# A hybrid attention encoder layer: eight landing buffers for stored block sums and u, low parts in halves, a merge ordered by token halves, and the second batch's mask loaded into memory that the first batch's u leaves

## The chip, the cores and the metric

The kernel runs on one core of one Trainium2 chip. The metric is the time of one execution on the device in microseconds (us), the median of several runs. Three runs of the kernel before gave 1134.05, 1135.88 and 1137.46 us; the median is 1135.88 us.

## The reference, cut to what matters

One encoder layer is applied to two request batches, the prompt (512 tokens) and the sample (1024 tokens), with the same weights, in float32. `D_MODEL` is 1024, and there are eight heads of 64 in each of two attention branches.

```python
def encoder_layer(x, ...):
    h = rmsnorm(x, norm_g)
    proj = h @ w_in                       # qa ka va za qb kb vb zb ga gb
    ...
    oa = neighbourhood_attention(qa, ka, va, rpb_a) * jax.nn.silu(za)   # window of 8 x 16 grid neighbours, bias per offset
    oa = oa @ w_o_a
    ob = window_gqa_attention(qb, kb, vb, t5_table, sink_b) * jax.nn.silu(zb)   # |i-j| <= 128, T5 bias, sink logit
    ob = ob @ w_o_b
    merged = jax.nn.sigmoid(ga) * oa + jax.nn.sigmoid(gb) * ob
    return x + merged @ w_out
```

`qa`, `ka`, `qb`, `kb` are normalised per head before the attention. In the kernel, u is the attention output times silu(z); g is the sigmoid of a gate.

## The kernel before

**Precision.** TensorE multiplies float32 operands that are split in two: a high part (the value as ScalarE writes it in the matmul's format) and a low part (the value minus the high part). Each product is three matmuls, high by high, high by low, low by high. ScalarE makes the high part (`whi`, `hh`, `T` first of a pair), VectorE or GpSimd the low part (`wlo`, `hl`, `T` second). Both parts of a pair of `T` tiles have the name `T` in the profile. So every operand passes DMA, then ScalarE, then VectorE or GpSimd, and then TensorE.

**Stages.** For each batch: norm, attention in six head groups (lines 607 to 1104: `att_weights`, `tables`, `project`, `make_qk`, `attend`, `weigh`), then `dense_phase`: z, the gates g, the merge with w_o_a and w_o_b, and the output product. The prompt's stages come first, and some of the sample's norm is done beside the prompt's dense phase. In the traced execution the prompt's attention runs to about 217 us, its dense phase to about 395 us, the sample's attention to about 785 us, and the sample's dense phase to the end.

**Attention.** `att_weights` loads four tiles of 768 columns for each group into `w` (the tag `w32`, two buffers), and makes `whi` and `wlo` of them; one instruction makes the whole low part. `project` multiplies h by them into a bank `p`; from it come the sums of squares, `rs_v` and `rs_r` on GpSimd, then `qk` on VectorE (line 816), which TensorE transposes (line 861). `tables` makes a table `bias` out of `mask` (one load, line 671) and `raw` (a load for each head, line 682) on VectorE or GpSimd (line 695). The scores need the table.

**Dense phase.** For the sample, z, g and the output use Strassen's seven products in place of eight (`pair_strassen`). Its operands from h are differences of four blocks of h. These block sums were stored to memory (`t_d`) beside the prompt's work and come back through `stored_sums`: each of 16 pieces is loaded to a landing buffer `U` (four buffers) and split into `T`. The u of each head pair, 16 pieces of 512 tokens, is stored to `u_d` and comes back through `split_u`, over two `fr` and two `ot` buffers. The merge takes the eight output blocks m and, inside each, the two token halves n, and needs u of that half. `fill_gates` are products of some gates that need only h; they are strewn into the sample's attention (`fh`, `fl`, bank `d`) to give TensorE something to do.

**What sets the order.** Every operation is put on record with a priority, its engine or choice of two engines, and the tiles that it makes and uses. `Flow.run` is a planner: with fixed cost formulas it plays the program through, and issues for each engine the ready operation with the smallest priority whose buffers are free. Where an operation may go to VectorE or GpSimd, it takes the one that it expects to end it sooner; operations with `port` don't overlap between those two engines in its plan. The order it finds is the program's: each engine takes its instructions strictly in that order, and waits where an operand or a buffer isn't there. The SyncE queue (SP) issues all DMAs in one order too, so a DMA that waits for its buffer or for the value it stores holds up all behind it.

**Memory.** `Stage` is a pool that is opened when others have been closed. The sample's `early` pool holds its q, k and small tiles and opens where the prompt's `u_p` was; its `late` pool holds `mask`, `raw`, `bias` and the rest of its attention, and opens when `norm_s`, `d1_p`, `rb`, `d0_p` and the prompt's h are closed.

Of the kernel before, what the change touches and what calls it, by code (L numbers as in the profile page):

```python
# [34 lines left out]
RAW = {512: 2, 1024: 1}  # L35
# [5 lines left out]
P = 128  # L41
# [313 lines left out]
def encoder_kernel(  # L355
# [238 lines left out]
    def att_weights(src, n, prio, engs=("pool", "dve"), place=None, after=()):  # L594

        st, at, new = place or (f.value(wpool, [P, 768], F32, "w32", W32), 0, True)
        hi = f.value(wpool, [P, 768], F32R, "whi", 6)
        lo = f.value(wpool, [P, 768], F32R, "wlo", 6)
        sv = lambda: st.t[:, at : at + n]
        ld = f.dma(lambda: nc.sync.dma_start(sv(), src), 512 * n, prio, after=after, **({"new": [st]} if new else {"hold": [st]}))  # L600
        a = f.op(
            (("act", ACT_(n) + 40),), lambda e: act.activation(hi.t[:, :n], sv(), AF.Copy),
            prio, new=[hi], hold=[st], after=[ld],
        )

        def emit(e):
            engines[e].tensor_tensor(lo.t[:, :n], sv(), hi.t[:, :n].bitcast(F32), op=ALU.subtract)
# [40 lines left out]
    def attention_phase(geo, hh, hl, h_ops, mask_d, early, late):  # L648
# [6 lines left out]
        def tile_(shape, dt, tag, bufs):  # L655
            return f.value(early if tag in ("sq", "ss", "rs_v", "rs_r", "v", "q", "qt", "qk") else late, shape, dt, tag, bufs)
# [479 lines left out]
    def dense_phase(geo, hh, hl, h_ops, o_stores, exps_done, start, opened, tp, up, p0, p1, p2, x_t, y_t, classic, fill, after_gates=None, side=None):  # L1136
# [93 lines left out]

        def stored_sums(prio, d, after):

            tv, ops = {}, {}
            for j in (1, 2, 0, 3):
                tv[j] = tuple(f.value(tp, [P, 4, nh], F32R, "T", 8) for _ in range(2))
                vh, vl = tv[j]
                for k in range(4):
                    st = tile_("U", 4)
                    dma(
                        lambda st=st, j=j, k=k: nc.sync.dma_start(st.t, d[j, k]), 512 * nh, prio, new=[st],  # L1240
                        after=after(j, k),
                    )
                    ops[j, k] = split(
                        lambda vh=vh, k=k: vh.t[:, k], lambda vl=vl, k=k: vl.t[:, k], lambda st=st: st.t, nh, prio,
# [79 lines left out]
        def pair_strassen(srcs, post, prio, mov_h, mov_t, seed=None, last=False, kept=None):  # L1324
# [40 lines left out]
            else:  # L1365
# [4 lines left out]
                result(0, 0, p1, mul(1, mov_h(1, 0)))  # L1370
            add(u2, p1, mul(2, mov_t(1)))
# [5 lines left out]
            if not last:  # L1377
                result(0, 1, u4, mul(6, mov_h(1, 1)))
                return
# [17 lines left out]

        def spare(tag):
            return f.value(wpool, [P, nh], F32, tag, {"fc": 1}.get(tag, 2))
# [271 lines left out]
        if not short:  # L1671
            for c in range(8):
                for n in halves:
                    st = f.value(wpool, [P, nh], F32, "fr", 2) if n else tile_("ot", n_ot)
                    dma(
                        lambda st=st, c=c, n=n: nc.sync.dma_start(st.t, u_d[c, :, half[n]]), 512 * nh, 10 + c // 4,
                        new=[st], after=stores["u", c, n],
                    )
                    split_u(c, n * nh, nh, st, 10 + c // 4)
# [20 lines left out]
        for q in range(8):  # L1700
            m = q if short else q // 2 + 4 * (q % 2)
            prio = 12 + q
            ws = []
            for br in range(2):
                raw = load_raw(w_g[m, 4 + br], prio - 2)
                ws.append(weight_tiles([raw], 4, prio - 0.5)[0])
            for n in halves:
                gs_ = []
                for br in range(2):
# [6 lines left out]
                    m_done[q, n] = product(ps, ws[br], movs, prio, True, True)  # L1716
                    tag, bufs = (("C", n_c), ("ot", n_ot) if short else ("U", 4))[br]
                    g = tile_(tag, bufs) if short or br or m < 4 else spare("fl" if n else "fh")
                    turn = [] if short or br or m < 4 else [m_done[max(q - 2, 0), 0]]
# [18 lines left out]
            if not short and m >= 4:  # L1738
# [109 lines left out]
    f.stage(-1000, (u_pool,), (early["s"],))  # L1848
    f.stage(-1000, (norm_s, d1["p"], rb_pool, d0["p"], r_h), (late["s"], d0["s"]))
# [92 lines left out]
```

## Time and profile before

| | |
|---|---|
| median of three runs | 1135.88 us |
| the profiled execution | 1136.88 us |
| its span, first to last instruction | 1135.1 us |
| between the two | 1.78 us |
| TensorE busy | 1121.6 us of the span |
| VectorE, ScalarE, GpSimd busy | 863.8, 653.7, 327.1 us |
| granted TensorE clock | 1.000 |

In a line of the timeline come the start in us, the busy time in us, the engine (PE TensorE, PEld its weight loads, DVE VectorE, ACT ScalarE, POOL GpSimd, SPq the DMA queue), the line of the kernel, the operation, output<-inputs, the shape, how many of them, and in brackets the idle time before it and what ended that. Matmuls are pipelined: one of 512 columns is shown with 0.39 us, but the next starts 0.23 us later, and one of 384 columns 0.17 us later. So a wait of TensorE is read from the step from one start to the next, less this usual step; the idle time in brackets is shorter, because the matmul before is drawn past its step.

### The profile page before, as it was taken

Reading aid. Unit: us, or ns where it says so; the run is one execution under the profiler, and the core shown is the slowest. Engines: PE = TensorE matmul, PEld = TensorE weight load, DVE = VectorE, ACT = ScalarE, POOL = GpSimd, SP = SyncE. Lnnn points to the kernel's source line nnn. Section 1 sums busy time; section 2 is a strip of 40 time slices with the busy share of each in tenths; the row PEclk is TensorE's granted clock in tenths of the full one; section 3 lists DMA queues with packets and bytes.
Section 4 is the critical chain, followed back from the end, with each engine's and each line's share of the span. In section 5 each row is a group of like instructions: output and inputs, shape, how many; then the busy total and the mean of one; then the engine's idle time right before and its main releaser. Section 6 shows DMA issues by size and latency. Waiting matters only on the chain.

```text
span 1135.1 us, 18686 instructions
## 1 busy us (share of the span) xinstructions
PE 1121.6 (99%) x6079; PEld 973.9 (86%) x6079; DVE 863.8 (76%) x1995; ACT 653.7 (58%) x1498; POOL 327.1 (29%) x432
## 2 busy tenths in 40 slices
PE   8999999999999999999999999999999999999998
PEld 6999988888888889999899988988788888788887
DVE  5888797587765468887868888885888866779874
ACT  6777987644433246574759888876534434522440
POOL 4654433000010044433414344420033221124221
PEclk9999999999999999999999999999999999999999
DMA  7854533488786422121312314244958645868982
GB/s 261 273 157 139 183 115 103 110 262 260 241 276 196 159 91 72 29 79 29 91 32 84 82 38 112 57 131 127 300 187 244 218 167 180 297 219 281 302 279 93
DMA packets 139108, 186.11 MB, mean 164 GB/s; under 512 B 29897, under 2 KB 68561, under 8 KB 139010
## 3 DMA queue, kind: packets, MB, share of 16 engines
q1 hardware_dynamic: 139010, 184.91, 51.4%
q8 instruction: 48, 0.79, 0.3%
q14 instruction: 50, 0.41, 0.1%
HBM read 138.71 MB, written 50.88 MB: 167 GB/s over the span
## 4 chain that ended last, share of the span: by engine, by line
PE 89%; DMA 4%; DVE 4%; ACT 1%; issue 1%; SPq 0%; POOL 0%; DVEq 0%; POOLq 0%; ACTq 0%
PE p L761 25%; PE x L1288 8%; PE x L1290 8%; PE x L1289 8%; PE x L1063 5%; PE x L1026 5%; PE x L934 5%; PE d L1288 4%; PE d L1289 4%; PE d L1290 4%; PE p L1289 4%; PE p L1290 4%; PE p L1288 4%; PE x L861 2%; DMA ot<-u_d 1%
## 5 line engine op out<-in xcount | busy, mean ns | idle before, releaser
L761 PE MATMUL p<-whi,hh 128*128 128x384 f32 x384 | 133.6, 348 | 0.0
L761 PE MATMUL p<-whi,hl 128*128 128x384 f32 x384 | 132.4, 345 | 0.0
L761 PE MATMUL p<-wlo,hh 128*128 128x384 f32 x384 | 132.2, 344 | 0.0
L978 ACT ACTIVATE sb<-sb,mx 128x384 f32<-128x384 f32 (+1 forms) x192 | 107.7, 565 | 22.9 <-DVE mx L969 22.6
L1170 ACT ACTIVATE whi<-raw 128x512 fp32r<-128x512 f32 (+1 forms) x136 | 79.4, 599 | 67.4 <-PE x L1289 46.3
L1289 PE MATMUL x<-T,whi 128*128 128x512 f32 x284 | 110.7, 390 | 0.3 <-DVE T L1175 0.2
L1288 PE MATMUL x<-T,whi 128*128 128x512 f32 x284 | 110.6, 390 | 0.0
L1290 PE MATMUL x<-T,wlo 128*128 128x512 f32 x284 | 110.5, 389 | 0.0
L761 PE MATMUL p<-whi,hb 128*128 128x384 f32 x384 | 107.8, 346 | 0.0
L1037 DVE TENSOR_TENSOR pp<-x,pp 128x512 fp32r<-128x512 f32 (+1 forms) x136 | 82.6, 639 | 20.3 <-ACT pp L1032 19.2
L1175 DVE TENSOR_TENSOR wlo<-raw,whi 128x512 fp32r<-128x512 f32 (+1 forms) x109 | 73.3, 682 | 26.5 <-ACT whi L1170 26.0
L1175 POOL TENSOR_TENSOR wlo<-raw,whi 128x512 fp32r<-128x512 f32 (+1 forms) x27 | 32.1, 1199 | 172.9 <-ACT whi L1170 160.2
L799 POOL TENSOR_TENSOR rs_r<-rs_v,mhalf 128x4 f32<-128x4 f32 (+1 forms) x72 | 79.9, 1109 | 5.7
L1032 ACT ACTIVATE pp<-x 128x512 fp32r<-128x512 f32 (+1 forms) x136 | 70.9, 561 | 18.2 <-PE x L1026 17.1
L792 POOL TENSOR_SCALAR rs_v<-ss 128x4 f32<-128x4 f32 (+1 forms) x72 | 26.0, 361 | 185.1 <-DVE ss L785 181.7
L1063 PE MATMUL x<-pp,v 128*128 128x256 f32 (+1 forms) x368 | 76.6, 322 | 0.0
L1288 PE MATMUL x<-hh,whi 128*128 128x512 f32 x196 | 76.4, 390 | 0.1
L1290 PE MATMUL x<-hh,wlo 128*128 128x512 f32 x196 | 76.3, 389 | 0.0
L1289 PE MATMUL x<-hl,whi 128*128 128x512 f32 x196 | 76.2, 389 | 0.0
L761 PEld LDWEIGHTS p<-whi,hl 128*128 128x128 f32 x384 | 72.8, 190 | 1.3 <-issue 1.0
L761 PEld LDWEIGHTS p<-whi,hh 128*128 128x128 f32 x384 | 73.0, 190 | 1.1 <-issue 0.5
L761 PEld LDWEIGHTS p<-wlo,hh 128*128 128x128 f32 x384 | 72.9, 190 | 0.9 <-issue 0.5
(381 smaller groups left out, 3011.9 us busy)
## 6 DMA issues: line engine op xcount, KB each, us to landing
raw<-in_w_g_dram SPq DMA_DIRECT2D x84, 256.0 KB
w<-in_w_att_dram SPq DMA_DIRECT2D x46, 384.0 KB
raw<-in_w_z_dram SPq DMA_DIRECT2D x40, 256.0 KB
ot<-o_d SPq DMA_DIRECT2D x36, 256.0 KB
raw<-in_w_out_dram SPq DMA_DIRECT2D x36, 256.0 KB
g_d<-C SPq DMA_DIRECT2D x34, 256.0 KB
fr<-in_w_g_dram SPq DMA_DIRECT2D x28, 256.0 KB
out_dram<-C SPq DMA_DIRECT2D x19, 256.0 KB
```

Source lines behind the costliest of these rows:

```text
L761: pe.matmul(ps.t[:, :GW], part[u](k), mv.t[:, c], start=k == 0 and m == 0, stop=k == KC - 1 and m == 2,)
L799: lambda e: nc.gpsimd.tensor_tensor(r.t[:, :nn], rv.t[:, :nn], mhalf[:, :nn], op=ALU.pow),
L934: pe.matmul(pss[2 * pair + i].t[:, :width], q.t[rows, u, at : at + P], kv[:, tiles[0] : tiles[-1] + 1 : step], start=n == 0, stop=n == 2,)
L978: act.activation(sb.t[:, :width], sb.t[:, :width], AF.Exp, bias=mx.t[:, i : i + 1], scale=-1.0, accum_out=sm.t[:, i : i + 1],)
L1032: lambda e, pt=pt, pp=pp, nn=nn: act.activation(pp.t[:, 0, :nn], pt.t[:, :nn], AF.Copy),
L1037: lambda e, pt=pt, pp=pp, nn=nn: dve.tensor_tensor(pp.t[:, 1, :nn], pt.t[:, :nn], pp.t[:, 0, :nn].bitcast(F32), op=ALU.subtract),
L1063: pe.matmul(out(), v.t[:, vs], mv(), start=first, stop=last)
L1170: (("act", ACT_(n)),), lambda e: act.activation(hi(), src(), AF.Copy), prio,
L1175: lambda e: engines[e].tensor_tensor(lo(), src(), hi().bitcast(F32), op=ALU.subtract), prio,
L1288: pe.matmul(out, hi.t[:, cs], mh(), start=first and k == 0, stop=False, **more)
L1289: pe.matmul(out, hi.t[:, cs], ml(), start=False, stop=False, **more)
L1290: pe.matmul(out, lo.t[:, cs], mh(), start=False, stop=last and k == len(ws) - 1, **more)
```

## The change

It has five parts.

1. **Landing buffers for block sums.** `stored_sums` lands the odd pieces of `t_d` in `fh` and `w32` buffers of the weight pool (two each), beside the four `U`. So eight are in flight.
2. **Landing buffers for u.** The 16 loads of u come by token half instead of by block, over `fr`, `fh`, `fl` and `ot` (two each, eight buffers).
3. **Merge by token halves.** The order of the merge is, for k = 0 to 3: half 0 of blocks k and k+4, then half 1 of both. Each block's weights are made once and kept for its two halves. In the first z pair of the sample the seventh product, which needs only h, is issued ahead of the products that need block sums.
4. **Low parts in halves.** `att_weights` makes each low part as two instructions of 384 columns, each with its own choice of VectorE or GpSimd.
5. **Mask and two bias tables.** For the sample, `mask` and `raw` (now two buffers instead of one) move to the `early` pool. That pool now opens when `u_p` and `norm_s` are closed, the `late` pool without waiting for `norm_s`.

```diff
-RAW = {512: 2, 1024: 1}
+RAW = {512: 2, 1024: 2}
...
-        def emit(e):
-            engines[e].tensor_tensor(lo.t[:, :n], sv(), hi.t[:, :n].bitcast(F32), op=ALU.subtract)
-
-        f.op(
-            tuple((e, {"pool": POOL_, "dve": DVE_}[e](n)) for e in engs), emit, prio, new=[lo], use=[hi], hold=[st], after=[a],
-        )
+        for i in range(2):
+            c = slice(i * n // 2, (i + 1) * n // 2)
+            f.op(
+                tuple((e, {"pool": POOL_, "dve": DVE_}[e](n // 2)) for e in engs),
+                lambda e, c=c: engines[e].tensor_tensor(
+                    lo.t[:, c], st.t[:, at : at + n][:, c], hi.t[:, c].bitcast(F32), op=ALU.subtract
+                ),
+                prio, use=[hi], hold=[st], after=[a], **({"into": [lo]} if i else {"new": [lo]}),
+            )
...
-            return f.value(early if tag in ("sq", "ss", "rs_v", "rs_r", "v", "q", "qt", "qk") else late, shape, dt, tag, bufs)
+            return f.value(early if tag in (("mask", "raw") if nt == NT_S else ()) or tag in ("sq", "ss", "rs_v", "rs_r", "v", "q", "qt", "qk") else late, shape, dt, tag, bufs)
...
+        def spare(tag):
+            return f.value(wpool, [P, nh], F32, tag, {"fc": 1}.get(tag, 2))
...
-                    st = tile_("U", 4)
+                    st = spare(("fh", "w32")[k // 2]) if not short and d is t_d and k % 2 else tile_("U", 4)
...
+            ps7 = mul(6, mov_h(1, 1)) if here and not prio else None
...
-                result(0, 1, u4, mul(6, mov_h(1, 1)))
+                result(0, 1, u4, ps7 or mul(6, mov_h(1, 1)))
...
-            for c in range(8):
-                for n in halves:
-                    st = f.value(wpool, [P, nh], F32, "fr", 2) if n else tile_("ot", n_ot)
+            for n in halves:
+                for c in range(8):
+                    st = spare(("fr", "fh", "fl")[c % 4]) if c % 4 < 3 else tile_("ot", n_ot)
+                    pr = 10 + n + c // 4 / 2
...
-        for q in range(8):
-            m = q if short else q // 2 + 4 * (q % 2)
-            prio = 12 + q
-            ws = []
-            for br in range(2):
-                raw = load_raw(w_g[m, 4 + br], prio - 2)
-                ws.append(weight_tiles([raw], 4, prio - 0.5)[0])
-            for n in halves:
+        turns, m_ws, m_prods = [(m, 0) for m in range(8)], {}, []
+        if not short:
+            turns = [(k + 4 * i, n) for k in range(4) for n in range(2) for i in range(2)]
+        for q, (m, n) in enumerate(turns):
+            if True:
+                prio = 12 + q * 8 / len(turns)
                 gs_ = []
+                if m not in m_ws:
+                    m_ws[m] = [
+                        weight_tiles([load_raw(w_g[m, 4 + br], prio - 2)], 4, prio - 0.5)[0] for br in range(2)
+                    ]
+                ws = m_ws[m]
...
-    f.stage(-1000, (u_pool,), (early["s"],))
-    f.stage(-1000, (norm_s, d1["p"], rb_pool, d0["p"], r_h), (late["s"], d0["s"]))
+    f.stage(-1000, (u_pool, norm_s), (early["s"],))
+    f.stage(-1000, (d1["p"], rb_pool, d0["p"], r_h), (late["s"], d0["s"]))
```

Since the planner settles the order, these edits move instructions on all engines. All 6076 matmuls are there before and after. The rows below are the program's order, with the line, the operation, output<-inputs and the shape; x2 means two equal ones; the line numbers are each kernel's own.

First, the SP queue at the sample's mask. `out_dram<-C` are the prompt's last output stores, `w_4890` and the like the sample's first attention weights, `fr` weights of `fill_gates`, `raw<-rpb_x` the rows that the tables are made of. Before:

```order
L1575 DMA out_dram<-C 128x512
L600 DMA w_4890<-in_w_att_dram 128x768
L1596 DMA fr<-in_w_g_dram 128x512
L682 DMA raw<-rpb_x_76 128x384
L671 DMA mask<-in_mask_s_dram 128x896
L1596 DMA fr<-in_w_g_dram 128x512
```

After, where `raw<-in_w_out` are weights of the prompt's output product and `C<-in_xt_p` its residual:

```order
L1258 DMA raw<-in_w_out_dram 128x512 x2
L1565 DMA C<-in_xt_p_dram 128x512
L1258 DMA raw<-in_w_out_dram 128x512
L685 DMA raw<-rpb_x_76 128x384 x2
L674 DMA mask<-in_mask_s_dram 128x896
L1258 DMA raw<-in_w_out_dram 128x512
```

The mask and two rows of the table go from behind the prompt's last stores to the middle of its output product, 29 rows of the queue earlier. On GpSimd, at the same place of the program, the table's pieces (`bias<-mask,raw`) stood between the first two tiles' `rs_v` and `rs_r`. Before:

```order
L792 TENSOR_SCALAR rs_v<-ss 128x4
L799 TENSOR_TENSOR rs_r<-rs_v,mhalf 128x4
L792 TENSOR_SCALAR rs_v<-ss 128x4
L695 TENSOR_TENSOR bias<-mask,raw 128x24x8
L799 TENSOR_TENSOR rs_r<-rs_v,mhalf 128x4
L695 TENSOR_TENSOR bias<-mask,raw 128x16x8
```

After:

```order
L795 TENSOR_SCALAR rs_v<-ss 128x4
L802 TENSOR_TENSOR rs_r<-rs_v,mhalf 128x4
L698 TENSOR_TENSOR bias<-mask,raw 128x24x8
L795 TENSOR_SCALAR rs_v<-ss 128x4
L802 TENSOR_TENSOR rs_r<-rs_v,mhalf 128x4
L698 TENSOR_TENSOR bias<-mask,raw 128x24x8 x4
```

Between the second `rs_v` and its `rs_r` no piece of the table stands any more. On TensorE twelve matmuls of `fill_gates` now stand ahead of the first transposes of `qk` there.

Second, the SP queue at the block sums of the sample's z, from the second group of four on. `ot<-o_d` are attention outputs, `u_d<-C` stores of u, `raw<-in_w_z` weights of z. Before:

```order
L1240 DMA U<-t_d 128x512 x3
L1527 DMA ot<-o_d_80 128x8x64 x2
L1512 DMA u_d_93<-C 128x512
L1252 DMA raw<-in_w_z_dram 128x512 x2
L1240 DMA U<-t_d 128x512 x4
L1527 DMA ot<-o_d_80 128x512 x2
L1512 DMA u_d_93<-C 128x512
L1252 DMA raw<-in_w_z_dram 128x512 x2
L1240 DMA U<-t_d 128x512 x4
```

After, where `w_10663` and the like are `w32` buffers:

```order
L1246 DMA w_10663<-t_d 128x512
L1246 DMA U<-t_d 128x512
L1246 DMA fh<-t_d 128x512
L1246 DMA U<-t_d 128x512
L1246 DMA w_10685<-t_d 128x512
L1531 DMA ot<-o_d_80 128x8x64 x2
L1516 DMA u_d_93<-C 128x512
L1258 DMA raw<-in_w_z_dram 128x512 x2
L1246 DMA U<-t_d 128x512
L1246 DMA fh<-t_d 128x512
L1246 DMA U<-t_d 128x512
L1246 DMA w_10767<-t_d 128x512
```

The third group of four now stands right behind the second, and the fourth where the third was.

Third, the SP queue where u is loaded ahead of the merge. `U<-g_d` and `C<-g_d` are stored gates, `g_d<-C` stores of the last gates. Before, four of the sixteen loads stand earlier, beside z and the first gates, and the other twelve from here on:

```order
L1676 DMA ot<-u_d_93 128x512 x2
L1252 DMA raw<-in_w_g_dram 128x512
L1676 DMA fr<-u_d_93 128x512 x2
L1676 DMA ot<-u_d_93 128x512
L1721 DMA U<-g_d_94 128x512 x2
L1676 DMA ot<-u_d_93 128x512
L1512 DMA g_d_94<-C 128x512
L1252 DMA raw<-in_w_g_dram 128x512
L1721 DMA U<-g_d_94 128x512
L1676 DMA fr<-u_d_93 128x512
```

After, the eight loads of half 0 stand earlier, beside z and the first gates, and the eight of half 1 begin at the same place:

```order
L1681 DMA fr<-u_d_93 128x512
L1681 DMA fl<-u_d_93 128x512
L1681 DMA ot<-u_d_93 128x512
L1258 DMA raw<-in_w_g_dram 128x512
L1681 DMA fr<-u_d_93 128x512
L1681 DMA fl<-u_d_93 128x512
L1729 DMA U<-g_d_94 128x512
L1681 DMA ot<-u_d_93 128x512
L1729 DMA U<-g_d_94 128x512
L1258 DMA raw<-in_w_g_dram 128x512
```

The last load of u stands 21 rows behind the first one of these before, and 14 rows behind it after.

More of the change, by code (lines that the diff above doesn't have):

```diff
@@ L1737, in dense_phase @@
                 m_vals[m, n] = a
-            if not short and m >= 4:
+            if not short and m >= 4 and n:
                 merged_sums(m - 4, prio)
```

16 lines of the change are left out of this document (7 added, 9 removed).

## The prediction

> **What bounds the kernel now.** I read the page's first part, then TensorE's waits, then the timeline around each place where its step from one matmul to the next is longer than usual.
>
> ```profile
> span 1135.1 us, 18686 instructions
> PE 1121.6 (99%) x6079; PEld 973.9 (86%) x6079; DVE 863.8 (76%) x1995; ACT 653.7 (58%) x1498; POOL 327.1 (29%) x432
> ...
> PE x L1799 <- DMA rb<-in_norm_row_dram: 4.6, 1, 4.6
> PE x L532 <- DVE xt L520: 0.6, 1, 0.6
> ```
>
> TensorE is busy for 1121.6 of 1135.1 us. The rows of waits give the sum, the count and the largest. The first is the load at the very start, which nothing here touches. The number of matmuls does not change, so all that can be gained or lost is waits of a few tenths up to 1.2 us, and a gain on another engine is worth only what TensorE waited for it. Four groups of these waits lie where the change works.
>
> **Part 5, mask and tables.** Around the sample's first transposes of `qk`, with the SP queue ahead:
>
> ```profile
> 351.06 0.33 SPq L1252 DMA_DIRECT2D raw<-in_w_out_dram  x1
> ...
> 400.94 0.43 SPq L671 DMA_DIRECT2D mask<-in_mask_s_dram  x1
> 405.96 0.71 POOL L695 TENSOR_TENSOR bias<-mask,raw 128x192 f32<-128x192 f32 x1 [1.86 <-DMA mask<-in_mask_s_dram]
> 406.64 1.06 POOL L799 TENSOR_TENSOR rs_r<-rs_v,mhalf 128x4 f32<-128x4 f32 x1
> 406.81 0.34 PE L761 MATMUL p<-whi,hl 128*128 128x384 f32 x1
> 407.73 0.42 DVE L816 TENSOR_TENSOR qk<-p,rs_r 128x256 f32<-128x256 f32 x1 [0.30 <-POOL rs_r L799]
> 408.21 0.44 PE L861 MATMUL x<-ident,qk 128*128 128x128 f32 x2 [1.06 <-DVE qk L816]
> ```
>
> The mask is issued at 400.94 and GpSimd waits 1.86 us for it with `bias`. Behind `bias` stands `rs_r`, and behind that `qk` and the transposes. TensorE's step 406.81 to 408.21 is 1.40 us, of which 0.17 is usual: a wait of 1.23. After, mask and two rows of the table stand among the weights of the prompt's output product, near the row at 351.06: 50 us earlier. Even if the two `raw` wait for their `early` buffers, they are there long before 405.96. No `bias` is between `rs_v` and `rs_r`, and twelve matmuls of `fill_gates` (12 x 0.23 = 2.7 us) stand ahead of the transposes. The moved DMAs are three issues of about 0.4 us on SP at a place where weights are loaded well ahead; their cover is that lead. Bounds: 0 (`rs_v` itself is late) to -1.23. I take -1.2, the upper end, because the wait's whole cause moves 50 us.
>
> **Part 4, low parts in halves.** The work by shapes, the stage by windows (length, then PE, PEld, DVE, ACT, POOL busy with counts, clock, DMA share, GB/s), and the place where a whole low part does harm:
>
> ```profile
> L607 DVE TENSOR_TENSOR wlo<-w,whi 128x768 fp32r<-128x768 f32 x34 | 32.6, 962 | 8.2 <-ACT whi L602 7.6
> L607 POOL TENSOR_TENSOR wlo<-w,whi 128x768 fp32r<-128x768 f32 x12 | 22.9, 1918 | 9.0 <-ACT whi L602 8.9
> L1175 DVE TENSOR_TENSOR wlo<-raw,whi 128x256 fp32r<-128x256 f32 x9 | 3.6, 414 | 0.0
> L1175 POOL TENSOR_TENSOR wlo<-raw,whi 128x256 fp32r<-128x256 f32 x7 | 5.8, 822 | 19.8 <-ACT whi L1170 19.8
> L1008 POOL TENSOR_TENSOR sb<-sb,rs 128x384 f32<-128x384 f32 x27 | 22.1, 832 | 31.2 <-DVE rs L1002 30.0 <-PE d L1290 1.2
> ...
> 406.00:785.00 379.00, 376.41 (x2419) 343.13 (x2418) 306.52 (x881) 272.58 (x702) 143.23 (x207) 1.00 0.25 68
> ...
> 546.35 0.42 DVE L1076 TENSOR_TENSOR ot__7030<-ot__7030 64x256 f32<-64x256 f32 x1 [0.66 <-ACT ot__7030 L1070]
> 547.12 3.81 POOL L607 TENSOR_TENSOR wlo<-w,whi 128x768 fp32r<-128x768 f32 x2 [0.26 <-ACT whi L602]
> 547.39 1.86 DVE L1080 TENSOR_TENSOR ot__7030<-ot__7030 64x256 f32<-64x256 f32 x1
> 548.39 0.34 PE L761 MATMUL p<-whi,hl 128*128 128x384 f32 x1
> 549.73 0.41 PE L861 MATMUL x<-ident,qk 128*128 128x128 f32 x2 [1.00 <-DVE qk L816]
> ```
>
> A half of 384 columns lies between the 256 and 768 columns of these rows: on VectorE a quarter of the way from 414 to 962 ns, 551; on GpSimd from 822 to 1918, 1096. In the order the 48 low parts (36 on VectorE, 12 on GpSimd) become 57 halves on VectorE and 39 on GpSimd. VectorE goes from 36 x 0.962 = 34.6 to 57 x 0.551 = 31.4 us, GpSimd from 23.0 to 39 x 1.096 = 42.7. GpSimd also takes 15 more scalings `sb` (832 ns each at most, +12.5). Both lie beside TensorE: in the sample's attention VectorE is busy for 306.5 of 379 us and GpSimd for 143.2. With that cover I cost the work itself at nothing. If the cover fails, every `wlo` late by a half costs up to 1.1 us of `project`.
>
> At 547.39 VectorE's `ot` of 64x256 takes 1.86 us, where a like one took 0.42 at 546.35. It ends at 549.25, when GpSimd's first whole low part (547.12 + 1.91) has just ended, and `qk` comes after it. TensorE's step 548.39 to 549.73 is 1.34, less 0.17: a wait of 1.17. With a half, GpSimd would be through at 547.12 + 1.10 = 548.22, 0.81 us sooner; if two halves follow each other on GpSimd, VectorE can come in between. Bounds 0 to -1.17; I take -0.8.
>
> This row also speaks against the change. In the Trainium skill, "SBUF — State Buffer", section "Who interferes with whom", a VectorE instruction with two SBUF inputs contends with a GpSimd instruction that reads SBUF, and whoever comes first may hold the other up for its whole length. By that rule more pieces on GpSimd mean more places where VectorE can be held, which makes a time of its own; the trace agrees as far as 1.86 against 0.42 us goes.
>
> As a mechanism of this kernel it is the third rival below: 42 more GpSimd pieces (27 halves, 15 scalings), each able to do what the row at 547.12 did.
>
> **Parts 1 and 3, block sums.** The SP queue, and TensorE's waits for `T`:
>
> ```profile
> 799.25 1.33 SPq L1240 DMA_DIRECT2D U<-t_d  x3
> 802.27 2.43 SPq L1512 DMA_DIRECT2D u_d<-C  x1
> 805.76 3.11 SPq L1240 DMA_DIRECT2D U<-t_d  x4
> 811.83 3.47 SPq L1240 DMA_DIRECT2D U<-t_d  x4
> ...
> 811.13 0.50 PE L1288 MATMUL x<-T,whi 128*128 128x512 f32 x1
> 811.85 0.50 PE L1289 MATMUL x<-T,whi 128*128 128x512 f32 x1 [0.22 <-DVE T L1175]
> 812.19 0.39 PE L1290 MATMUL x<-T,wlo 128*128 128x512 f32 x1
> ...
> 814.50 0.39 PE L1288 MATMUL x<-T,whi 128*128 128x512 f32 x1
> 815.00 0.50 PE L1289 MATMUL x<-T,whi 128*128 128x512 f32 x1
> ...
> 818.99 0.39 PE L1288 MATMUL d<-T,whi 128*128 128x512 f32 x1
> 819.73 0.50 PE L1289 MATMUL d<-T,whi 128*128 128x512 f32 x1 [0.35 <-DVE T L1175]
> ...
> 822.35 0.39 PE L1288 MATMUL d<-T,whi 128*128 128x512 f32 x1
> 823.17 0.50 PE L1289 MATMUL d<-T,whi 128*128 128x512 f32 x1 [0.43 <-DVE T L1175]
> ```
>
> Steps of 0.72, 0.50, 0.74 and 0.82 us, each less 0.23, are waits of 0.49, 0.27, 0.51 and 0.59, together 1.86. The step behind such a wait is long too (811.85 to 812.19 is 0.34, +0.11), four times: 0.44. That makes 2.30 us. The third group of loads goes out at 805.76, behind a store of u that blocks the queue for 2.43 us; the fourth at 811.83. After, the third group stands right behind the second (799.25 + 1.33 = 800.6), 5 us earlier, and the fourth where the third was, 6 us earlier; both are more than the largest wait. The change puts nothing into the place except that the `w32`, `fh` buffers belong to other users: weights that the attention and the fills have used up by then. The moved product of h (`ps7`, three times four matmuls of 0.23 us) gives 2.7 us more lead. Bounds 0 (the store or the splits hold, not the buffers) to -2.30; I take -2.3, since 5 us are ten times what is missing. VectorE's splits of the earlier loads come beside its attention work; late next would be the store of u, for which nobody waits until the merge.
>
> **Parts 2 and 3, u and the merge.** The first pieces of the sample's merge:
>
> ```profile
> 969.73 0.39 PE L1290 MATMUL p<-T,wlo 128*128 128x512 f32 x1
> 970.37 0.49 PE L1288 MATMUL p<-T,whi 128*128 128x512 f32 x1 [0.25 <-ACT T L1170]
> 971.10 0.50 PE L1289 MATMUL p<-T,whi 128*128 128x512 f32 x1 [0.23 <-DVE T L1175]
> ```
>
> Steps of 0.64 and 0.73, less 0.23 each: 0.41 + 0.50, and 0.10 behind them, 1.01 us. After, half 0 is loaded beside z and the first gates, and half 1 is wanted only after the first two blocks' products of half 0 (48 matmuls x 0.23 = 10.9 us later). Its loads begin at the same place and end 14 rows of the queue on instead of 21. Bounds 0 to -1.01; I take -1.0. Block weights kept for two halves are made once as before: 0.
>
> **What is added.** The planner's order changes everywhere, also in the prompt, where all low parts are halved. New waits can't be read from the trace before; the nearest rows are the 0.6 of `xt` above and this one in an undisturbed stretch of attention, step 0.63 less 0.17:
>
> ```profile
> 421.12 0.34 PE L761 MATMUL p<-whi,hl 128*128 128x384 f32 x1
> 421.75 0.81 PE L1026 MATMUL x<-ident,sb 128*128 128x128 f32 x4 [0.29 <-DVE sb L1010]
> ```
>
> Bounds -1.1 (these two vanish) to +2.9 (as much as attention has now: 1.23 + 0.46 + 1.17). I take one more such wait, +0.6.
>
> **The sum.** -1.2 - 0.8 - 2.3 - 1.0 + 0.6 = -4.7 us. The execution in the profile took 1136.9 us (span 1135.1 and 1.8 around it): 1132.2 after. The median of the runs, 1135.9, lies 1.0 below it, so 1131.2. A difference under 0.3% (3.4 us) can't be told from none here.
>
> **The rivals.**
> First, the new order gives the waits back. The planner works with fixed costs and knows nothing of held engines; the two waits at 408 and 549 are of the kind that it did not foresee. If the attention again has 2.9 us of waits and the start another 0.6, the added term is 3.5 instead of 0.6: -1.8, 1134.1 us, no change. For it: all of attention is re-planned. Against it: over 379 us the old order had only three such places.
> Second, the shared buffers or the queue hold the early loads. If `w32` and `fh` come free late, or the store at 802.27 blocks what now stands behind it, the 2.3 and 1.0 stay: -1.4, 1134.5 us, no change. Against it: the third group no longer stands behind that store.
> Third, slower: GpSimd holds VectorE, as at 547.12. One hit is worth at most a half's length less what `ot` needs on its own time, about 1.10 - 0.24 = 0.86 us. Of 63 pieces before (12 low parts, 51 scalings) one hit reached TensorE. It ends above +3.4 us from (4.7 + 3.4) / 0.86 = 10 hits among the 42 added pieces, about one in four; at one in three, 14 hits, 12.0 - 4.7 = +7.3, 1143.2 us.
> Fourth, part 5 does not do what it says: mask or `raw` wait for their `early` buffers until the old place. Then -3.5 remains, 1132.4 us, at the bound of faster.
>
> **How the numbers follow.** The forecast 0.53, the first rival 0.24, the second 0.10, the third 0.09, the fourth 0.04. The forecast's own range goes from all waits named here gone (1.23 + 0.46 + 0.6 + 1.17 + 2.30 + 1.01 = 6.8, 1129.1) to +1.5 on its sum, 1132.7. The whole range: at the low end 1129.1 less some of the spread of the runs (1.7 to either side), 1128.0; at the high end the first two rivals, 1134.5, with that spread, 1136.2, and the third with six or seven hits (-4.7 + 5.6 = +0.9, 1136.8): 1137.0. Faster than 1132.5 are nearly all of the forecast and half of the fourth: 0.54. Slower is the third's larger part and a little of the first: 0.09. The rest, 0.37, is no change.
>
> **What would show it.** Right: the mask issued near 351 us and no wait for it on GpSimd at the sample's start; no wait of TensorE for `T` between 805 and 830 and at the first products of the merge; no VectorE instruction of over 1.3 us beside a low part on GpSimd. TensorE's waits in all would be some 5 us smaller at 1121.6 us of busy time. Wrong: waits for `qk` or `sb` at new places in either attention, VectorE instructions stretched beside halves, or `U` loads that still go out after 805.

## The result and the profile after

| | before | after |
|---|---|---|
| median of the runs | 1135.88 us | 1148.10 us (1144.76 to 1149.21, 5 runs) |
| ratio of the runs | 1 | 1.0106, 95% interval 1.0088 to 1.0124 |
| profiled execution, its span | 1136.88, 1135.1 us | 1149.21, 1147.4 us |
| granted TensorE clock in it | 1.000 | 0.997 |

The change made the kernel 12 us slower; 1131.2 was forecast, and a range up to 1137.0. Busy time and TensorE's waits after (sum, count and largest of each):

```profile
span 1147.4 us, 18752 instructions
PE 1126.2 (98%) x6079; PEld 975.1 (85%) x6079; DVE 863.7 (75%) x1993; ACT 656.1 (57%) x1495; POOL 372.7 (32%) x485
...
PE x L1807 <- DMA rb<-in_norm_row_dram: 4.5, 1, 4.5
PE p L1295 <- DVE hl L1178: 2.7, 1, 2.7
PE x L1294 <- ACT hh L1173: 2.3, 1, 2.3
PE d L1295 <- DVE T L1178: 1.7, 3, 0.9
PE x L864 <- DVE qk L819: 1.6, 2, 0.9
PE x L1029 <- DVE sb L1013: 1.4, 2, 0.7
PE d L1294 <- DVE fc L1612: 1.1, 2, 0.8
PE p L1295 <- DVE T L1178: 1.0, 2, 0.7
PE p L764 <- DVE hb L667: 0.7, 1, 0.7
```

VectorE works as long as before (863.7 and 863.8 us), GpSimd 45.6 us more. TensorE's idle time grew from 13.5 to 21.2 us, and its busy time by 4.6 us, although it does the same work. Most of these 4.6 us are two stretches of 3.41 us at half the clock, one right behind each of its two longest waits:

```profile
357.57:360.98 3.41, 1.39 (x7) 0.76 (x5) 2.96 (x5) 1.29 (x3) 1.29 (x1) 1.00 0.66 163
360.98:364.39 3.41, 3.14 (x7) 2.22 (x8) 2.45 (x4) 1.37 (x3) 0.00 (x0) 0.50 0.89 273
1067.54:1070.95 3.41, 0.69 (x3) 0.61 (x4) 3.41 (x4) 0.63 (x1) 2.11 (x2) 1.00 0.15 57
1070.95:1074.36 3.41, 3.41 (x10) 2.66 (x9) 2.59 (x5) 0.00 (x0) 0.00 (x0) 0.50 0.46 153
```

Each row is a stretch of the changed kernel: its length, then PE, PEld, DVE, ACT and POOL busy, the granted clock, the DMA share and GB/s. At a clock of 0.50, matmuls of 512 columns start 0.43 us apart instead of 0.23, and the two stretches cost 1.7 and 1.6 us. The trace before has no such stretch ahead of its last matmul.

Both profiles count 6079 matmuls (three more than the 6076 given above), so the start of the n-th of them cuts both traces at the same amount of work. The stages in us, each from the start of one of these matmuls to the start of another:

| matmuls | what is in it | before | after | difference |
|---|---|---|---|---|
| from 1 to 1350 | prompt's attention, first z | 225.3 | 228.5 | +3.2 |
| to 2072 | prompt's z, gates, merge, output | 163.6 | 167.9 | +4.3 |
| to 4550 | sample's attention | 389.6 | 389.1 | -0.5 |
| to 4831 | sample's z | 66.3 | 67.2 | +0.9 |
| to 5561 | gates, u, first merge turns | 166.5 | 166.1 | -0.4 |
| to the last | last merge turns, output | 115.7 | 120.7 | +5.0 |

The prompt's attention loses its 3.2 us in no single place: TensorE has five waits of 0.7 to 0.8 us there (two for `sb`, one each for `fc`, `hb` and `qk`), where it had two of 0.5 and 0.6 before. Three places carry the rest. **The last merge turn**, where TensorE waits for `hl` of `fl`. After:

```profile
1066.52 1.47 POOL L1178 TENSOR_TENSOR T<-U,T 128x512 fp32r<-128x512 f32 x1 [1.15 <-ACT T L1173]
1066.78 1.75 DVE L1167 TENSOR_TENSOR S<-raw,S 128x512 f32<-128x512 f32 x1
1067.94 1.71 POOL L1167 TENSOR_TENSOR S<-raw 128x512 f32<-128x512 f32 x1
1068.45 1.75 DVE L1178 TENSOR_TENSOR hl<-fl,hh 128x512 fp32r<-128x512 f32 x1
1070.26 0.50 PE L1295 MATMUL p<-hl,whi 128*128 128x512 f32 x1 [2.74 <-DVE hl L1178]
```

Before, the same work at the same place (its matmul is the one at 1059.85, 0.22 us late):

```profile
1058.52 0.68 DVE L1175 TENSOR_TENSOR T<-U,T 128x512 fp32r<-128x512 f32 x1
1059.12 0.68 DVE L1175 TENSOR_TENSOR hl<-fl,hh 128x512 fp32r<-128x512 f32 x1
```

Two VectorE instructions in a row take 1.75 us instead of 0.68, each drawn out to about 0.55 us behind the end of the GpSimd instruction that had begun before it. Together they lose 2.1 of the 2.7 us. The half clock behind the wait adds about 1.6, which makes most of the stage's 5.0.

**The prompt's output product.** The last gate load of the prompt's merge, its activation, the last `hh`, and the output product's first matmul, after and before:

```profile
351.28 0.33 SPq L1729 DMA_DIRECT2D ot<-g_d  x1
354.02 0.39 PE L1294 MATMUL x<-hh,whi 128*128 128x512 f32 x1
354.26 0.63 ACT L1509 ACTIVATE ot<-ot 128x512 f32<-128x512 f32 x1 [1.29 <-DMA ot<-g_d]
360.57 0.63 ACT L1173 ACTIVATE hh<-C 128x512 fp32r<-128x512 f32 x1 [2.12 <-DVE C L1167]
361.25 0.79 PE L1294 MATMUL x<-hh,whi 128*128 128x512 f32 x1 [2.29 <-ACT hh L1173]
```

```profile
343.59 1.17 SPq L1721 DMA_DIRECT2D ot<-g_d  x1
347.35 0.63 ACT L1505 ACTIVATE ot<-ot 128x512 f32<-128x512 f32 x1 [2.60 <-DMA ot<-g_d]
350.92 0.39 PE L1288 MATMUL x<-hh,whi 128*128 128x512 f32 x1
353.04 0.63 ACT L1170 ACTIVATE hh<-C 128x512 fp32r<-128x512 f32 x1 [1.47 <-DVE C L1164]
```

Counted from the output's first matmul, the gate load went out 7.3 us ahead before and 2.7 after, and the last `hh` began 2.1 us behind it before and 6.6 after. It is needed by the eighth product, 7 x 0.68 = 4.8 us behind the first. The wait and the half clock behind it make nearly all of the stage's 4.3 us.

**The block sums.** After, the third group of loads and TensorE's waits:

```profile
808.44 0.38 SPq L1246 DMA_DIRECT2D U<-t_d  x1
815.07 1.29 POOL L1167 TENSOR_TENSOR S<-raw,S 128x512 f32<-128x512 f32 x1 [30.36 <-ACT T L1173]
815.09 1.82 DVE L1178 TENSOR_TENSOR T<-U,T 128x512 fp32r<-128x512 f32 x1 [0.15 <-ACT T L1173]
816.90 1.76 POOL L1178 TENSOR_TENSOR wlo<-raw,whi 128x512 fp32r<-128x512 f32 x1 [0.54 <-ACT whi L1173]
816.96 0.50 PE L1295 MATMUL d<-T,whi 128*128 128x512 f32 x1 [0.91 <-DVE T L1178]
817.43 1.77 DVE L1178 TENSOR_TENSOR T<-fh,T 128x512 fp32r<-128x512 f32 x1
819.26 0.50 PE L1295 MATMUL d<-T,whi 128*128 128x512 f32 x1 [0.64 <-DVE T L1178]
```

Counted from the stage's start (matmul 4550, 783.1 before and 790.0 after), the third group goes out at 18.4 us instead of 22.7 (805.76): 4.2 us earlier. But the splits `T` take 1.8 us each beside GpSimd's `S` and `wlo`.

### The profile page after: what moved, and what is told of

Read it like the earlier page. It is cut to its first block, busy times and chain, and to the rows that moved or that the text cites. A ratio compares the mean times of both kernels' runs of the same rounds, so it can differ in the third digit from the quotient of the medians.

```text
span 1147.4 us, 18752 instructions
## 1 busy us (share of the span) xinstructions
PE 1126.2 (98%) x6079; PEld 975.1 (85%) x6079; DVE 863.7 (75%) x1993; ACT 656.1 (57%) x1495; POOL 372.7 (32%) x485
## 4 chain that ended last, share of the span: by engine, by line
PE 83%; DMA 6%; DVE 5%; issue 2%; ACT 2%; POOL 1%; SPq 1%; DVEq 0%; POOLq 0%; ACTq 0%
PE p L764 23%; PE x L1294 8%; PE x L1295 8%; PE x L1296 8%; PE x L1066 5%; PE x L1029 5%; PE x L937 4%; PE d L1294 3%; PE p L1295 3%; PE d L1296 3%; PE d L1295 3%; PE p L1296 3%; PE p L1294 3%; PE x L864 2%; DMA w<-in_w_att_dram 1%
## 5 line engine op out<-in xcount | busy, mean ns | idle before, releaser
L1178 POOL TENSOR_TENSOR wlo<-raw,whi 128x512 fp32r<-128x512 f32 (+1 forms) x29 | 39.0, 1349 | 221.4 <-ACT whi L1173 221.4
L764 PE MATMUL p<-whi,hb 128*128 128x384 f32 x384 | 110.1, 349 | 0.7 <-DVE hb L667 0.7
L1295 PE MATMUL x<-T,whi 128*128 128x512 f32 x280 | 108.9, 389 | 0.0
L1294 PE MATMUL x<-T,whi 128*128 128x512 f32 x280 | 108.9, 389 | 0.0
L1295 PE MATMUL x<-hl,whi 128*128 128x512 f32 x200 | 78.5, 392 | 0.0
L1029 PE MATMUL x<-ident,sb 128*128 128x128 f32 x496 | 71.1, 274 | 2.0 <-DVE sb L1013 1.4
```

The source lines that it names most:

```text
L764: pe.matmul(ps.t[:, :GW], part[u](k), mv.t[:, c], start=k == 0 and m == 0, stop=k == KC - 1 and m == 2,)
L1029: pe.transpose(pt.t[:, u * P : (u + 1) * P], sbs[i].t[:, c * P : (c + 1) * P], ident)
L1178: lambda e: engines[e].tensor_tensor(lo(), src(), hi().bitcast(F32), op=ALU.subtract), prio,
L1294: pe.matmul(out, hi.t[:, cs], mh(), start=first and k == 0, stop=False, **more)
L1295: pe.matmul(out, hi.t[:, cs], ml(), start=False, stop=False, **more)
```

## The experiments

Each was timed beside the kernel before, on one chip. The stages are those of the table above, from one profiled execution each. Ten traces besides that of before have its order in the first stage (e2 to e7, e9 to e12), and there it took 223.6 to 226.0 us: a difference of up to 2 us in that stage is spread. The profiled execution can also lie off the median: it is the slowest of its kernel in after, e1, e3 and e11 (1.1, 1.2, 3.3 and 3.4 us above the median) and the fastest in e10 (2.9 below).

| run | median us | ratio to before, 95% interval | stages us |
|---|---|---|---|
| e1 halves alone | 1139.98 | 1.0035 (1.0022 to 1.0048) | 230.2, 165.8, 387.4, 65.6, 166.7, 115.7 |
| e2 mask alone | 1137.42 | 1.0012 (1.0000 to 1.0024) | 225.9, 163.6, 387.1, 69.0, 166.4, 115.5 |
| e3 parts 1, 2, 3 | 1140.99 | 1.0050 (1.0037 to 1.0063) | 226.0, 163.6, 389.3, 66.8, 165.8, 123.1 |
| e4 without halves | 1143.05 | 1.0064 (1.0051 to 1.0077) | 223.6, 163.7, 386.9, 70.4, 166.4, 121.4 |
| e5 merge order alone | 1142.55 | 1.0050 (1.0030 to 1.0071) | 224.9, 164.2, 388.9, 67.1, 166.3, 121.8 |
| e6 e5, no GpSimd there | 1138.16 | 1.0025 (1.0013 to 1.0037) | 225.6, 163.6, 388.8, 66.5, 166.1, 117.5 |
| e7 halves, sample only | 1134.26 | 0.9988 (0.9977 to 0.9999) | 225.2, 163.7, 387.3, 65.6, 166.6, 116.2 |
| e8 prompt halves on VectorE | 1137.57 | 1.0021 (1.0008 to 1.0035) | 229.4, 163.8, 386.8, 65.6, 166.4, 116.3 |
| e9 block sums alone | 1136.18 | 1.0002 (0.9993 to 1.0012) | 225.1, 164.0, 389.5, 67.3, 166.3, 115.6 |
| e10 e9, no GpSimd there | 1135.65 | 0.9994 (0.9984 to 1.0004) | 224.4, 163.6, 389.0, 64.0, 166.3, 115.7 |
| e11 three causes away | 1135.89 | 1.0003 (0.9991 to 1.0015) | 225.1, 163.7, 388.6, 68.8, 165.8, 117.3 |
| e12 candidate | 1131.18 | 0.9961 (0.9948 to 0.9974) | 224.7, 163.6, 387.7, 63.7, 165.9, 115.6 |
| e13 halves, same order | 1135.48 | 0.9996 (0.9987 to 1.0005) | 225.4, 163.7, 388.4, 66.0, 166.0, 115.3 |
| e14 halves, measured cost | 1147.98 | 1.0113 (1.0097 to 1.0130) | 228.5, 171.0, 389.6, 66.5, 166.4, 116.0 |

In these traces stretches of 3.41 us at half clock lie in the first stage of e1 and of e8, in the second of e14, in z of e4 (two in a row) and e11, and in the last stage of e3, e4 and e5. Each makes its stage up to 1.7 us longer (half of 3.41). The other traces have none ahead of their last matmul.

**Which part loses where (e1 to e4).** e1 is the kernel before with this piece of the change, e4 the changed kernel without it:

```diff
+        for i in range(2):
+            c = slice(i * n // 2, (i + 1) * n // 2)
...
+                tuple((e, {"pool": POOL_, "dve": DVE_}[e](n // 2)) for e in engs),
```

e2 is the kernel before with the two lines on `mask` and `RAW` and the stages:

```diff
-RAW = {512: 2, 1024: 1}
+RAW = {512: 2, 1024: 2}
...
-    f.stage(-1000, (u_pool,), (early["s"],))
+    f.stage(-1000, (u_pool, norm_s), (early["s"],))
```

e3 has the rest: the landing buffers, u, the merge order and the moved product.

```diff
+                    st = spare(("fh", "w32")[k // 2]) if not short and d is t_d and k % 2 else tile_("U", 4)
...
+            ps7 = mul(6, mov_h(1, 1)) if here and not prio else None
...
+                    st = spare(("fr", "fh", "fl")[c % 4]) if c % 4 < 3 else tile_("ot", n_ot)
...
+            turns = [(k + 4 * i, n) for k in range(4) for n in range(2) for i in range(2)]
```

> The kernel before with part 4 alone (low parts in two halves). Up to the sample's mask its order is that of the changed kernel. Theory H (the halves delay the prompt): TensorE has the changed kernel's waits in the prompt, 3.3 us up to 150 us and 4.2 us at the output product near 361 us, and none of before's 1.2 us at 549: about 1142 us. Rival Q (mask and table rows in the queue at 360 make the wait at 361): only the 3.3 us, about 1138.5 us. Rival L (all waits come from the mixture of the parts): within 2 us of 1136.

> The kernel before with part 5 alone (mask and two table rows early). Its prompt is that of before up to the mask. H: the prompt has no new wait, the 1.2 us at 408 go or come back as the 1.0 us that the changed kernel has there, the re-planned attention adds -1 to +1: 1135 to 1137 us. Q: a wait of some 4 us at the prompt's output product, about 1140 us.

> The kernel before with parts 1, 2 and 3 (landing buffers, u by token halves, merge order), without 4 and 5. Up to 760 us its order is that of before. H and Q: the 1.2 us that the changed kernel lost at the block sums and the 4.9 us at the end of the merge are here too, u gains 0.4: about 1141.5 us. L: these waits need the other parts; -3 us as forecast, about 1133 us.

> The changed kernel without part 4 (whole low parts). H: the prompt's 7.5 us are gone, the rest stays: about 1140.5 us. Q: 3.3 us are gone, the 4.2 at 361 stay: about 1144.5 us. L: between 1136 and 1148, with no rule.

The prompt's loss comes with the halves and goes with them: its two stages are 7.1 us longer than before in e1 (of which up to 1.7 is half clock) and no longer in e4, where the 1.6 us less is spread. TensorE's longest waits up to 405 us, behind the load at the very start, in e1 and then in e4:

```profile
PE x L1294 <- ACT hh L1173: 1.4, 1, 1.4
PE d L1294 <- DVE fc L1611: 0.8, 1, 0.8
PE x L864 <- DVE qk L819: 0.7, 1, 0.7
PE x L937 <- ACT qt L899: 0.6, 1, 0.6
```

```profile
PE x L861 <- DVE qk L816: 0.5, 1, 0.5
```

The wait at the output product stands in e1, which has no early mask, and not in e2 and e4, which have it: rival Q falls. The merge's loss stands in e3 and e4: it needs no halves. L, by which e1 would have stayed within 2 us of 1136 and e3 have come to about 1133, falls too. That 4.6, 2.0 and 5.6 us above 1135.4 in e1 to e3 make 12.2, as much as the whole change lost, is partly luck: by stages the parts don't add up (the sample's attention is 2.2, 2.5 and 0.3 us shorter in e1 to e3, but 0.5 shorter in the whole change). e1 came out 2 us lower than H said, since the halved attention of the sample gained 2.2. e2 gained 2.5 there without halves, more than the 1.2 us forecast, and lost 2.7 in z, on which no theory had counted; its seven executions at a granted clock of 1.000 took 1134.1 to 1137.6 us, the five below it 1138.1 to 1140.7. e4 lies 2.5 us above H: its z has two stretches at half clock, behind waits for `T` from 807 us on.

**The merge (e5, e6).** e5 is the kernel before with the lines on `turns` alone. e6 adds, in the planner's test of whether an operation may start:

```diff
         def barred(o, e):
+            if e == "pool" and o.port and 1039500 <= now < 1060000:
+                return True
```

> The kernel before with part 3's merge order alone, without the moved product of h and without parts 1, 2, 4, 5; its matmuls stand in the same order as before. Theory K (the new merge order puts the last turn's fl, hh, hl behind VectorE instructions that GpSimd holds): the waits of 0.7 and 2.9 us at the last merge turn and the following ones are all here, +5 us: about 1140.5 us. Rival D (they come from the early loads of u and block sums): no new wait, about 1135.5 us.

> The kernel of e5 in which, in the planner's stretch of 20 us that holds the last merge turns, work that may go to VectorE or GpSimd goes to VectorE alone (four GpSimd instructions fewer there). K with the hold as cause: no VectorE instruction is stretched there, the wait for the last hl falls from 2.9 to under 0.7 us, about 1136.5 us. Rival C (the last turn's chain is too long, or VectorE is full): the wait stays or grows, with VectorE's four added instructions (2.7 us of work), 1140 us or more.

The merge order alone makes the loss, although its matmuls stand in the same order as before. In e6 the place reads:

```profile
1058.25 0.69 DVE L1166 TENSOR_TENSOR S<-raw,S 128x512 f32<-128x512 f32 x1
1058.86 0.68 DVE L1177 TENSOR_TENSOR hl<-fl,hh 128x512 fp32r<-128x512 f32 x1
1059.60 0.50 PE L1294 MATMUL p<-hl,whi 128*128 128x512 f32 x1 [0.37 <-DVE hl L1177]
```

VectorE does more work there, yet both instructions take 0.68 us (1.75 in e5) and the wait is 0.37 us where e5 had 2.6 and the changed kernel 2.7. The half clock that follows this wait in e5 is gone as well. The stage falls from 121.8 to 117.5 us, the median by 4.4. So the hold, with the half clock behind it, is the larger part of the merge's loss. Two of e5's seven executions had a granted clock of 1.000; they took 1138.4 us, as long as e6's median, and the other five 1141.3 to 1145.7. Some 1.8 us, which e6's stage has above before, are not explained by the hold; the trace has most of it in two waits of the output product for `fh`.

**The halves in the prompt (e7, e8, e13, e14).** In e7 only the sample's low parts are halved, in e8 the prompt's halves are given to VectorE alone:

```diff
+        parts = 2 if f.base else 1
+        for i in range(parts):
```

```diff
+                tuple((e, {"pool": POOL_, "dve": DVE_}[e](n // 2)) for e in (engs if f.base else ("dve",))),
```

> Part 4 alone, but the prompt's low parts stay whole and only the sample's are halved. Theory H (halves harm the prompt and help the sample): the prompt as before, the sample's attention and z as in e1, -2.9 us: about 1132.5 us. Rival N (what the sample gained in e1 was only a better chance of order): between 1135 and 1138 us.

> Part 4 alone with the prompt's halves on VectorE only (the sample's on either). H, if GpSimd's long halves make the prompt late (a weight buffer is held until its second half, 2.0 us after the first on GpSimd, is read): the waits at 70 to 150 us and at 361 go, about 1136 us. H, if halving itself is the cause (VectorE pays twice the fixed part, 24 x 0.14 = 3.4 us more): they stay or grow, 1140 to 1142 us.

e7 leaves the prompt as before and keeps the gain in the sample's attention (387.3): 0.9988, about half of the 2.9 us expected, and between what its two theories said. e8 also came between its two numbers: the wait at the output product is gone (163.8), but the prompt's attention stays at 229.4, of which up to 1.7 is half clock. So GpSimd's share is not the whole of it, and I was left with halving itself or the order. e13 issues both halves inside the planner's one operation, so that every other instruction stands where it stood before; e14 gives the planner the measured prices:

```diff
+            for i in range(2):
+                c = slice(i * n // 2, (i + 1) * n // 2)
+                a = engines[e].tensor_tensor(lo.t[:, c], st.t[:, at : at + n][:, c], hi.t[:, c].bitcast(F32), op=ALU.subtract)
```

```diff
-                tuple((e, {"pool": POOL_, "dve": DVE_}[e](n // 2)) for e in engs),
+                tuple((e, {"pool": 1010, "dve": 550}[e]) for e in engs),
```

> Each low part as two instructions of 384 columns, one behind the other on the engine that before had the whole; every other instruction of every engine in the order of before. If halving itself costs (fixed part twice, on the prompt's tightly used VectorE): prompt some 4 us later as in e1, about 1139.5 us. If the new order is the cause: 36 x 0.14 = 5 us more VectorE work that is hidden, within 1 us of before, 1135 to 1137 us.

> Part 4 alone (as e1), with a half costed to the planner at 0.55 us on VectorE and 1.01 on GpSimd in place of 0.47 and 0.95. If the cost formula is the cause of the prompt's waits: they fall by half or more, 1135 to 1137 us. If it is the finer order as such, which no cost mends: 1139 to 1141 us as e1.

e13 takes 1135.48 us, no change: halving as such costs nothing. It also shows that a half does what the prediction said at its place near 549. The `ot` that took 1.86 us there takes 1.03, and TensorE's idle time falls from 1.00 to 0.19 us, by the 0.8 forecast:

```profile
547.23 1.03 DVE L1083 TENSOR_TENSOR ot__7070<-ot__7070 64x256 f32<-64x256 f32 x1
548.74 0.41 PE L864 MATMUL x<-ident,qk 128*128 128x128 f32 x2 [0.19 <-DVE qk L819]
```

e14, with better prices, is as slow as the whole change, and loses nearly all of it in the prompt (228.5 and 171.0, together 10.6 us above before, up to 1.7 of it half clock); neither of its theories had that. So the loss in the prompt belongs to the order in which the planner strings the halves, its choice of engine included, and a better price did not mend it. Which swap of rows makes the gate loads late is open; that it ends in `hh` waiting behind an `ot<-g_d` load is read from the trace only.

**The block sums (e9, e10).** e9 is the kernel before with the lines on `t_d` and `ps7`; e10 adds the test of e6 for 795000 to 811000.

> The kernel before with part 1 and the moved product of h alone. Forecast theory (loads go out 5 us earlier, so the 2.3 us of waits for T go): about 1133.5 us. Theory K (the loads are earlier, but the splits T then meet GpSimd's S and low parts, and VectorE is held): waits for T of 2 to 3 us in all stay, about 1136 us.

> The kernel of e9 in which work that may go to either engine goes to VectorE alone in the planner's 16 us around the first two z pairs (six GpSimd instructions). K: no held T there, the waits fall under 1 us in all, 1133.5 to 1134.5 us. If VectorE's amount of work or the landing of the loads is what counts: 2 to 4 us of waits, 1136 to 1138 us.

In e9 TensorE's waits in z, between 780 and 858 us, are:

```profile
PE d L1292 <- DVE T L1175: 1.6, 1, 1.6
PE p L1292 <- DVE T L1175: 0.9, 2, 0.7
```

The waits of before are replaced by others, at splits that GpSimd holds. In e10's trace no such wait is left, and the stage is 64.0 us, 2.3 below before: the gain that was forecast. The timed runs don't confirm it: e10's median is 0.5 us below e9's, less than the intervals are wide, and its profiled execution (1132.8 us) is the fastest of its 12. So the trace shows that GpSimd held the splits, but a gain from it is not shown. What the other executions lost is open.

**Together (e11, e12).** e11 is the whole change with the prompt's low parts whole and GpSimd barred as in e6 at both places:

```diff
+            if e == "pool" and o.port and (799000 <= now < 811000 or 1039500 <= now < 1064000):
+                return True
```

e12 has part 1, `ps7`, part 2, halves in the sample only and the bar of e10, but neither the merge order nor the early mask.

> All five parts, but the prompt's low parts whole (part 4 in the sample only), and work that may go to either engine on VectorE alone in the planner's 12 us at the first two z pairs and its 24 us at the last merge turns. If the three places named explain the loss: 1148.1 less 5 (prompt, from e4), less 4.4 (merge, e5 to e6), less 1 to 3 (z): 1136 to 1138 us. If something else of the mixture counts: over 1140 us.

> A candidate for a version that beats both: part 1, the moved product, the early loads of u (part 2, with the merge order of before), low parts in halves in the sample only, and VectorE alone in the planner's 16 us at the first two z pairs. From e7 -1.5 us, from e10 up to -2, from u -0.8: 1131.5 to 1134 us. If gains don't add: 1134 to 1137 us.

e11 comes back to before (1135.89), 12.2 us under the changed kernel. By its stages the prompt (-7.6 us against after) and the last stage (-3.4) did it. Its z is 68.8 us, 1.6 more than in after, about what its stretch at half clock costs. TensorE's waits for `T` fell there from 2.4 to 0.5 us, but waits for weights (`whi`, `wlo`), 1.7 us, took their place, so the bar at the block sums gained nothing in this mixture. e12 is faster than both kernels: 0.9961 (0.9948 to 0.9974), 4.7 us under before and 16.9 under after, and 0.3 below the range expected. Which of its parts earns how much is not shown, since e12 without the bar was not run. TensorE's waits in it:

```profile
PE x L1807 <- DMA rb<-in_norm_row_dram: 4.7, 1, 4.7
PE x L867 <- DVE qk L822: 1.3, 2, 0.8
PE x L1032 <- DVE mx L975: 0.5, 1, 0.5
```

## Why the prediction was wrong

- **What is added, +0.6 with a bound of +2.9.** This is the term that failed. It priced the new order by the waits of the old one, in the sample's attention and at the start. It named the prompt, but gave it no price beyond the 0.6 of `xt`, and the merge none. The trace after has +7.5 us in the prompt and +5.0 in the last stage. e13 shows that the order and not the instructions makes the prompt's part; which rows of the order do it stays open.
- **The clock, left out.** All that could be lost was said to be waits, each at its length. The two waits of over 2 us were each followed by 3.41 us at half clock, about 3.3 us in all, and TensorE was busy for 1126.2 us instead of the 1121.6 expected.
- **Merge order, cost 0.** Wrong by 5.0 us in the last stage of after and by 6.1 in that of e5. The step spoke of lead for u and of weights made once; it did not follow `fl`, `hh`, `hl` of the last turn, which was 0.2 us late already before, and it priced no half clock.
- **Block sums, -2.3.** The third group did go out 4.2 us earlier, as said. The step failed where it took the splits as hidden work: they are the path, and GpSimd held them (0.9 us lost in after; e9 no change).
- **The third rival, 0.09.** Its mechanism, GpSimd holding VectorE, was right, and it was right that it ends on the slow side. It was sized wrongly: 0.86 us a hit and ten hits. In the merge two hits on one chain cost 2.7 us and the half clock behind them 1.6, and the hits were not on the added pieces but on old ones that the new order laid beside each other.
- **Mask and tables, -1.2.** The mask was issued at 360.70, 40 us earlier, and the wait for it is gone. A new one of 1.05 us took its place, shown in the last section. In e2 the re-planned attention gained 2.5 us and z lost 2.7.
- **Low parts, -0.8.** Right at its place: e13, in the old order, takes 0.8 us off the wait near 549. That the halves make the whole gain of e7's attention, 2.3 us, is not shown: e2 gains 2.5 there with whole low parts. A half took 0.60 us on VectorE and 1.06 on GpSimd, where 0.55 and 1.10 had been worked out:

```profile
L610 DVE TENSOR_TENSOR wlo<-w,whi 128x384 fp32r<-128x384 f32 x53 | 30.3, 599 | 10.0 <-ACT whi L602 9.5
L610 POOL TENSOR_TENSOR wlo<-w,whi 128x384 fp32r<-128x384 f32 x39 | 40.7, 1056 | 54.7 <-ACT whi L602 54.1 <-PE x L1066 0.5
```

- **u, -1.0.** Half at most: the stage is 0.4 us shorter in after (166.1) and 0.8 in e3 (165.7), but the runs without this part lie between 166.0 and 166.8 too.

## What to carry to other kernels

Where a planner sets the order, an edit that adds or resizes operations is a new draw of the whole order: price it by what the order does on every chain that already has less than a microsecond to spare, and not by the edit's own instructions (that this would have caught the loss was not tried). A wait that leaves TensorE idle for half of 3.41 us costs more than its length here, because half clock follows. Test the instructions with the old order (e13) and each part alone, by stages cut at equal counts of matmuls, before the mixture. Of two engines that hold each other, take the helping one out of the few stretches where the path runs through the other. At the merge that took 4.4 us off the median (e6 against e5), at the block sums nothing that the times confirm (e10 against e9). e12, which has it there beside the parts that help, is 0.4% faster than before.

## What the runs showed of the hardware

**Half clock behind a wait.** I cut the traces of both kernels and of e1 to e14 into stretches of 3.41 us, from the first entry of the clock's record to the last matmul. Eleven stretches are at half clock. In nine of the eleven cases TensorE had been idle for 0.50 to 0.82 of the stretch right before; in the other two, in the prompt's attention of e1 and e8, for 0.35 and 0.29. Every stretch that was idle for half or more was followed by half clock, and the idlest one that was not is at 0.46 (e5, at 1090 us). e6 shows it as an experiment: with the wait of e5 cut from 2.6 to 0.37 us, the half clock behind it is gone. No run varied the length of such a wait by itself.

**A hold in both directions.** The hold between VectorE and GpSimd goes both ways, and a run of short instructions can hold a long one. At the sample's start, after:

```profile
407.31 4.74 POOL L1178 TENSOR_TENSOR fl<-fr,fh 128x512 fp32r<-128x512 f32 x1 [48.01 <-ACT fh L1173]
408.65 2.24 DVE L698 TENSOR_TENSOR bias<-mask,raw 128x128 f32<-128x128 f32 x10
412.41 1.01 POOL L802 TENSOR_TENSOR rs_r<-rs_v,mhalf 128x4 f32<-128x4 f32 x1
413.45 0.42 DVE L819 TENSOR_TENSOR qk<-p,rs_r 128x256 f32<-128x256 f32 x1 [2.55 <-POOL rs_r L802]
413.93 0.44 PE L864 MATMUL x<-ident,qk 128*128 128x128 f32 x2 [0.89 <-DVE qk L819]
```

GpSimd's instruction of 128x512 takes 1.29 us at 815.07; here it takes 4.74 and ends 1.2 us behind VectorE's ten table pieces; `rs_r`, `qk` and the transposes come after it. In the Trainium skill, "SBUF — State Buffer", section "Who interferes with whom", a VectorE instruction with two SBUF inputs contends with a GpSimd instruction that reads SBUF, and the one that comes first may hold the other up for its whole length. The trace agrees that either can be held: at 1066.52 GpSimd's instruction was first, and at 407.31 VectorE was already at a cast, begun at 407.11. That a whole run of pieces holds one GpSimd instruction is this trace's addition, read from this one place.
